# A decoder trunk on one core: the bias rows of one head group stored once, the even mixer and the last tail in another order, and a pair's scores computed in two halves of the array

## The chip, the core and the metric

The kernel runs on one core of one Trainium2 chip. The core has five engines with instruction streams of their own: TensorE (PE; the profile lists its weight loads apart, as PEld), VectorE (DVE), ScalarE (ACT), GpSimd (POOL) and SyncE (SP), which here only issues DMAs. The metric is device microseconds of one execution. Three runs of the kernel before gave 584.12 us as their median (583.64 to 584.29). The profiled execution took 583.38 us; its span, from the first to the last thing that the profiler recorded, is 581.6 us, so 1.8 us lie around it.

## The reference, cut to what matters

256 tokens of width 1024, four residual layers, each with an RMSNorm in front:

- an even mixer: one input projection; half of its output goes through a double-gated convolution of width 3, half through causal pooling means over 2, 4, 8 and 16 tokens with a linear map per group; both halves are concatenated and projected back;
- a gated MLP of 2816 with a causal convolution of width 3 before SiLU;
- an odd mixer: 16 heads of width 64. Heads 0 to 7 add a difference of cumulated forget gates to the logits, heads 8 to 15 add a bias by distance, `rel_bias[bucket(q - k)]` (T5's buckets). All are causal. The softmax over keys and the product with the values follow, then the output projection;
- a second gated MLP, and a last RMSNorm over each token.

For heads 8 to 15 the bias of query q and key k depends on q - k alone, so one row of 256 numbers per head holds all of it.

## The kernel before, in words

Everything is float32. Each operand of a large product is split into a rounded part (`hi`, type fp32r) and a rest (`lo`), and three products replace one: hi·hi, hi·lo, lo·hi (`mm3`, L276). Weights come in blocks of 128x1024: SP issues the DMA into `st` (eight buffers), ACT casts it to `hi` (L133), DVE subtracts it for `lo` (L134); seven pairs of buffers hold the split blocks. `ahead()` (L154) keeps six blocks on the way beyond the one in use, in the order of the list `blocks`, which is written out at L73 to L121.

The order of PE's instructions is the order of the program (`manual_schedule` with `ORDERED`). The order on ACT, DVE and POOL is set by a planner, except in the first loads (L257) and in the end of the kernel (`ordered_final`, L845), where ACT and DVE keep the order of the program too.

**Even mixer** (L396 to L512). Four groups j of 128 channels. `even_in("x", j)` and `even_in("y", j)` project; from the results `pool_sums`, `pool_less` and `pool_map` make `yb[j]`, and `conv_half` makes `ya[j]`. `even_add(j)` adds the output projection of `ya[j]` and then of `yb[j]`, 24 matmuls each. The PSUM pool `psA` hands out four banks in turn.

**First MLP** (`ffn`, L517). Its `aside` is `t5_rows` (L584): a small matmul makes the bias rows of the eight heads, DVE copies them into `row` (8 partitions x 384, the last 128 columns a large number), and POOL issues one DMA that writes each row 128 times into DRAM (`rowd`, 8x128x384).

**Odd mixer** (L600 to L813). Heads go in pairs p. `pair_bias` (L661) reads a 128x2x256 tile per pair: for heads 8 to 15 from `rowd` with a step of 383 per partition, so that each partition sees its row shifted by one. `queries` and `keys` project with 24 matmuls of 256 columns each. `part_keys` (L696) splits the keys of both heads into the tile `kz`, in which the other head's 64 partitions are zero (memsets at L693, L694, on POOL). `scores` (L702) then runs three matmuls of 512 columns (queries 128 to 255, both heads' 256 keys side by side) and three of 256 (queries 0 to 127, 128 keys each). DVE adds the bias and takes the extreme (L716, L718), ACT takes exponentials. Two pairs later PE transposes the result (`turn`, L733), and `mix` (L745) multiplies it by the values, one head into partitions 0 to 63 of `po` and one into 64 to 127.

**End** (`final`, L816). The last MLP accumulates by token: `acc.t[i][n]` holds tokens 128i to 128i+127 and columns 512n to 512n+511. The last two blocks of the output weights are kept as `tail`; for i and n in turn the tail's products close a bank, ACT squares and sums it (L834), DVE multiplies by the norm's weights (L836), and after n = 1 the row's scale is made (L838, L839 on POOL), applied (L840 on DVE, L841 on ACT) and the halves are sent (L842 on ACT's queue, L843 on SP's).

Of the kernel before, what the change touches and what calls it, by code (L numbers as in the profile page):

```python
# [11 lines left out]
F32 = mybir.dt.float32  # L12
# [27 lines left out]
SPLIT = 7  # L40
LOOK = 6
LEAD = 8
FIRST = LEAD + T + 512

# [6 lines left out]
def trunk(ctx, tc, a, out):  # L51
# [25 lines left out]

    def even_in_blocks(j):
        for n, kind in enumerate("xy"):
            for q in range(2):  # L80
                block(("e" + kind, j, q), a["ev_in"][GROUPS[j], n, :, q * BLK:(q + 1) * BLK])

    def even_out_blocks(j):
        block(("eo", j), a["ev_out"][GROUPS[j]])
        block(("eo", j + NG), a["ev_out"][GROUPS[j] + NG])

    for j in range(1, NG):
        even_in_blocks(j)
        if j >= 2:
            even_out_blocks(j - 2)  # L90
    even_out_blocks(NG - 2)
    even_out_blocks(NG - 1)

    def ffn_blocks(l):
        for kind, f in ffn_steps:
# [5 lines left out]
        for f in (NF - 2, NF - 1):  # L101
            block(("fo", l, f), a["ff_out"][l, f])
# [293 lines left out]
    with tc.tile_pool(name="ev", bufs=2) as ev, tc.tile_pool(name="evc", bufs=1) as evc:  # L396
# [46 lines left out]

        def even_add(j, between=None):
            acc.add_all(weights(("eo", j)), ya[j])
            if between is not None:
                between()
            acc.add_all(weights(("eo", j + NG)), yb[j])

# [45 lines left out]
        ahead()  # L495
        even_add(0, lambda: pool_map(1))
        ahead()
        zx = even_in("x", 3)
        pool_sums(3, zx[:, 0, :])
        pool_map(2)  # L500
# [16 lines left out]
    def ffn(l, st, hg, ps_z, ps_acc, kind_acc, end, aside=None):  # L517
        with tc.tile_pool(name=f"ff{l}", bufs=2) as fp:
            acc = None
            ready = {}  # L520
            rrow = None
            z0 = None

# [22 lines left out]

            for kind, f in ffn_steps:
# [30 lines left out]
            tail = [(weights(("fo", l, k)), ready.pop(k)) for k in (NF - 2, NF - 1)]  # L578
            return end(acc, tail)


    rowd = drp.tile([NH, P, 384], F32, name="rowd")

    def t5_rows(ps):  # L584
# [15 lines left out]
    with tc.tile_pool(name="od", bufs=2) as od, tc.tile_pool(name="odc", bufs=1) as odc:  # L600
# [60 lines left out]
        def pair_bias(p):  # L661

            b = od.tile([P, 2, T], F32, tag="bias", name="bias", bufs=3)
            if p < 4:
                s = fd[:, :]
                src = bass.AP(tensor=s.tensor, offset=s.offset + 2 * p * T, ap=[[0, P], [T, 2], [1, T]])
            else:
                s = rowd[:, :, :]
# [22 lines left out]
        kzs = [odc.tile([P, 2, 2, T], F32R, name=f"kz{i}") for i in range(2)]  # L691
        for kz in kzs:
            nc.gpsimd.memset(kz[HD:, :, 0, :].bitcast(F32), 0.0)  # L693
            nc.gpsimd.memset(kz[:HD, :, 1, :].bitcast(F32), 0.0)  # L694

        def part_keys(kz, kf):  # L696
            for s in range(2):
                r = slice(s * HD, (s + 1) * HD)
                nc.scalar.copy(kz[r, 0, s, :], kf[r, :])
                nc.vector.tensor_sub(kz[r, 1, s, :], kf[r, :], kz.bitcast(F32)[r, 0, s, :])  # L700

        def scores(qs, kz, bias):  # L702

            pr2 = []
            sums = []
            ps1 = psB.tile([P, 2, T], F32, tag="ps", name="ps_s1")
            ps0 = psB.tile([P, 2, T], F32, tag="ps", name="ps_s0")
            for n, (x, y) in enumerate(((0, 0), (0, 1), (1, 0))):
                nc.tensor.matmul(ps1, qs[x][:, P:], kz[:, y], start=n == 0, stop=n == 2)
            for n, (x, y) in enumerate(((0, 0), (0, 1), (1, 0))):  # L710
                nc.tensor.matmul(ps0[:, :, :P], qs[x][:, :P], kz[:, y, :, :P], start=n == 0, stop=n == 2)
            for s in range(2):
                n1, n0 = bias[s]
                lg = od.tile([P, 384], F32, tag="lg", name="lg")
                mx = od.tile([P, 2], F32, tag="mx", name="mx")
                nc.vector.tensor_tensor_reduce(lg[:, :T], ps1[:, s, :], n1, 1.0, 3e38, op0=ALU.add, op1=ALU.min,  # L716
                                               accum_out=mx[:, 0:1])
                nc.vector.tensor_tensor_reduce(lg[:, T:], ps0[:, s, :P], n0, 1.0, 3e38, op0=ALU.add, op1=ALU.min,  # L718
                                               accum_out=mx[:, 1:2])
# [43 lines left out]

        def keys(p, kz, between=None):
# [8 lines left out]
        qs, pr, pb, turned = {}, {}, {}, {}  # L773

        def score(i):
            pr[i] = scores(qs.pop(i), kzs[i % 2], pb.pop(i))

# [8 lines left out]
        for i, p in enumerate(order):  # L786
            pb[i] = bias_of(p)
            qs[i] = queries(p, lambda: turn_at(i - 2))
            if i >= 1:
                score(i - 1)  # L790
            keys(p, kzs[i % 2], lambda: mix_at(i - 2))
            if i == 0:
# [23 lines left out]
    def final(acc, tail):  # L816
        with tc.tile_pool(name="fin", bufs=1) as fin:
# [10 lines left out]

            for i in range(2):
                r, v = rcol[:, i:i + 1], var[:, i:i + 1]  # L830
                for n in range(2):
                    for m, (w, y) in enumerate(tail):
                        acc.add(i, n, w, y, m == len(tail) - 1)
                    nc.scalar.activation(junk, acc.t[i][n], AF.Square, accum_out=sums[:, i, n:n + 1])  # L834
                    if n == 0:
                        nc.vector.tensor_mul(hg_[:, i, :], acc.t[i][0], gb[:, :512])  # L836
                        nc.vector.tensor_scalar(v, sums[:, i, 0:1], 1.0 / D, EPS, op0=ALU.mult, op1=ALU.add)
# [22 lines left out]
def _layout(i):  # L860
# [40 lines left out]
    hot = np.zeros((32, T), np.float32)  # L901
    hot[_t5_bucket()[::-1], np.arange(T)] = -1.0
    a["hot"] = hot
# [20 lines left out]
```

## Time and profile before

| what | value |
|---|---|
| median of three runs | 584.12 us (583.64 to 584.29) |
| profiled execution | 583.38 us |
| its span | 581.6 us |
| granted clock of TensorE, mean over the span | 0.994 |
| ACT busy, DVE busy | 350.3 us, 453.8 us |
| PE's share of the chain that ended last | 71% |
| matmuls | 3696 |

Busy time of PE is from modelled ends of pipelined matmuls: one row's duration overlaps the next. What a matmul costs is read from the distance between starts. `L301` is line 301 of the kernel; `zg<-hg,hi` is the tile written and the tiles read, buffer numbers left out; `128*128` are the rows and columns of the array in use; "idle before" names what ended an engine's idle time. The granted clock is 1.00 at 2.4 GHz and 0.50 at 1.2 GHz.

### The profile page before, as it was taken

To read this page: it belongs to the slowest core of one execution; us is meant where nothing else is said; L and a number is where in the kernel's file an instruction comes from. 1 tells how busy PE (TensorE), PEld (TensorE's weight loads), DVE (VectorE), ACT (ScalarE), POOL (GpSimd) and SP (SyncE) were. 2 spreads that over 40 slices of the span, in tenths; PEclk is the share of its full clock that TensorE was granted. 3 is DMA by queue.
4 is the path that set the end of the run, shared out by engine and by line. 5 is a ranking of instruction groups with operands and counts; after the bars stand their busy time and mean duration, and the time that the engine had idled before them with its cause. 6 is when DMAs were issued, how large, how long until landed. Compare 5 with 4: busy or idle time off the path is not lost.

```text
span 581.6 us, 9818 instructions
## 1 busy us (share of the span) xinstructions
PE 568.8 (98%) x3696; PEld 512.4 (88%) x3696; DVE 453.8 (78%) x784; ACT 350.3 (60%) x618; POOL 79.1 (14%) x91
## 2 busy tenths in 40 slices
PE   8999999998999999999999999999999999999995
PEld 7999998997999999999888999998888888888883
DVE  6999698944999777878688888578977787887752
ACT  7764476623667555557567776566755556555532
POOL 1531051000000000004171347031000000000000
PEclk9999999998999999999999999999999999999998
DMA  8966636578777655655656443447465555656001
GB/s 311 405 219 202 233 117 215 90 138 249 265 237 220 190 188 186 190 185 152 228 179 185 159 152 112 147 142 245 156 197 195 181 188 183 189 187 202 1 2 72
DMA packets 30896, 106.00 MB, mean 182 GB/s; under 512 B 4112, under 2 KB 4376, under 8 KB 30848
## 3 DMA queue, kind: packets, MB, share of 16 engines
q1 hardware_dynamic: 28944, 100.61, 52.8%
q0 software_dynamic: 1616, 4.24, 4.2%
q8 instruction: 29, 0.48, 0.3%
q10 hardware_dynamic: 288, 0.52, 0.2%
q14 instruction: 19, 0.16, 0.1%
HBM read 102.72 MB, written 2.63 MB: 181 GB/s over the span
## 4 chain that ended last, share of the span: by engine, by line
PE 71%; issue 9%; DMA 7%; DVE 6%; POOL 4%; ACT 1%; SPq 0%; POOLq 0%; ACTq 0%
PE zg L301 12%; PE zu L301 12%; PE zg L302 6%; PE zu L302 6%; DMA st<-in_ff_out 5%; PE acc L278 4%; PE acc L279 4%; PE acc L277 4%; PE ta L279 3%; PE ta L278 3%; PE ta L277 3%; DVE lo L134 2%; POOL nb L677 1%; PE pv L615 1%; PE pv L617 1%
## 5 line engine op out<-in xcount | busy, mean ns | idle before, releaser
L134 DVE TENSOR_TENSOR lo<-st,hi 128x1024 fp32r<-128x1024 f32 (+1 forms) x186 | 230.2, 1246 | 80.5 <-ACT hi L133 79.3
L133 ACT CAST hi<-st 128x1024 fp32r<-128x1024 f32 (+1 forms) x186 | 191.9, 1039 | 124.8 <-PE acc L278 22.0
L301 PE MATMUL zg<-hg,hi 128*128 128x512 f32 x352 | 127.9, 401 | 2.5 <-DVE zs L533 2.5
L301 PE MATMUL zu<-hg,hi 128*128 128x512 f32 x352 | 126.3, 397 | 0.3 <-DVE hg L197 0.3
L302 PE MATMUL zg<-hg,lo 128*128 128x256 f32 x352 | 99.3, 282 | 0.0
L302 PE MATMUL zu<-hg,lo 128*128 128x256 f32 x352 | 98.7, 280 | 0.0
L301 PEld LDWEIGHTS zg<-hg,hi 128*128 128x128 f32 x352 | 66.7, 190 | 18.5 <-DVE zs L533 2.8
L301 PEld LDWEIGHTS zu<-hg,hi 128*128 128x128 f32 x352 | 66.1, 188 | 15.9 <-DVE hg L197 0.6
L302 PEld LDWEIGHTS zu<-hg,lo 128*128 128x128 f32 x352 | 66.6, 189 | 0.8
L302 PEld LDWEIGHTS zg<-hg,lo 128*128 128x128 f32 x352 | 67.2, 191 | 0.0
L279 PE MATMUL acc<-y_h,lo 128*128 128x256 f32 x176 | 49.6, 282 | 0.0
L277 PE MATMUL acc<-y_h,hi 128*128 128x256 f32 x176 | 49.6, 282 | 0.0
L278 PE MATMUL acc<-y_l,hi 128*128 128x256 f32 x176 | 49.5, 281 | 0.0
L310 ACT CAST y_h<-y 128x256 fp32r<-128x256 f32 x44 | 17.8, 406 | 38.3 <-DVE y L544 38.3
L388 ACT ACTIVATE t<-zs,vec 128x256 f32<-128x256 f32 x44 | 26.4, 601 | 15.7 <-DVE zs L537 15.7
L217 POOL TENSOR_TENSOR sqs<-sq 128x512 f32<-128x512 f32 x4 | 5.2, 1294 | 223.9 <-ACT sq L212 223.9
L277 PE MATMUL ta<-hi,y_h 128*128 128x512 f32 x88 | 34.8, 395 | 0.0
L279 PE MATMUL ta<-hi,y_l 128*128 128x512 f32 x88 | 34.7, 395 | 0.0
L278 PE MATMUL ta<-lo,y_h 128*128 128x512 f32 x88 | 34.7, 395 | 0.0
L277 PEld LDWEIGHTS acc<-y_h,hi 128*128 128x128 f32 x176 | 33.1, 188 | 0.8
L279 PEld LDWEIGHTS acc<-y_h,lo 128*128 128x128 f32 x176 | 33.2, 188 | 0.0
L278 PEld LDWEIGHTS acc<-y_l,hi 128*128 128x128 f32 x176 | 33.1, 188 | 0.0
(222 smaller groups left out, 1211.3 us busy)
## 6 DMA issues: line engine op xcount, KB each, us to landing
st<-in_ff_in SPq DMA_DIRECT2D x88, 512.0 KB, 4.4
st<-in_ff_out SPq DMA_DIRECT2D x44, 512.0 KB, 4.3
st<-in_od_qk SPq DMA_DIRECT2D x16, 512.0 KB, 4.3
st<-in_ev_in SPq DMA_DIRECT2D x10, 512.0 KB, 7.1
st<-in_ev_out SPq DMA_DIRECT2D x8, 512.0 KB, 3.9
st<-in_od_v SPq DMA_DIRECT2D x8, 512.0 KB, 3.6
st<-in_od_out SPq DMA_DIRECT2D x8, 512.0 KB, 3.9
first<-in_first SPq DMA_DIRECT2D x7, 388.0 KB, 6.0
```

What stands on the lines that cost most here:

```text
L133: nc.scalar.copy(hi[:, s:e], st[:, s:e])
L134: nc.vector.tensor_sub(lo[:, s:e], st[:, s:e], hi.bitcast(F32)[:, s:e])
L277: nc.tensor.matmul(o, wh, xh, start=start, stop=False, skip_group_check=skip)
L278: nc.tensor.matmul(o, wh, xl, start=False, stop=False, skip_group_check=skip)
L279: nc.tensor.matmul(o, wl, xh, start=False, stop=stop, skip_group_check=skip)
L301: nc.tensor.matmul(z, wh, x[:, k], start=first, stop=False, skip_group_check=True)
L302: nc.tensor.matmul(z[:, 1, :], wl, x[:, k, 0, :], start=False, stop=last, skip_group_check=True)
L310: nc.scalar.copy(hi, src)
L388: nc.scalar.activation(t, u, AF.Identity, scale=col(w0 + 2), bias=bias)
L615: nc.tensor.matmul(pv[i], xh, wh, start=k == 0, stop=False)
L617: nc.tensor.matmul(pv[i], xl, wh, start=False, stop=k == NK - 1)
L677: nc.gpsimd.tensor_scalar(nb[:, T:], fbh[:, :P], fq[:, hh:hh + 1], None, op0=ALU.subtract)
```

## The change

Four things. The T5 rows are written once (`rowd` is 8x384), with the large number in front and the row's distances rising behind it; each partition q reads from offset q on, which gives the keys last first, and DVE reads the tile backwards. In the even mixer the output projections of `ya[j]` and `yb[j]` are added separately, and the x projection of group 3 runs between those of group 0; the weight blocks follow that order. The last MLP keeps three blocks for the tail (`TAIL`), and in the end the first bank of tokens 128 to 255 is closed before tokens 0 to 127 are scaled and sent, both halves of which then go out on SP's queue. `scores` no longer uses `kz`: the keys are split once for both heads (`split`), and each head's products use only its own 64 partitions, into a bank of its own.

```diff
@@ even mixer's blocks and program
+    even_in_blocks(1)
+    even_in_blocks(2)
+    even_out_block(0)
+    even_in_blocks(3, "x")
+    even_out_block(NG)
+    even_in_blocks(3, "y")
     for j in range(1, NG):
...
+        even_out_block(j)
+        even_out_block(j + NG)
...
-        even_add(0, lambda: pool_map(1))
-        ahead()
+        even_add(0)
+        pool_map(1)
         zx = even_in("x", 3)
         pool_sums(3, zx[:, 0, :])
+        ahead()
+        even_add(NG)
         pool_map(2)
-        ahead()
         zy = even_in("y", 3)
         conv_half(3, zx, zy)
         pool_less(3)
         ahead()
         even_add(1)
+        even_add(NG + 1)
         pool_map(3)
-        ahead()
         even_add(2)
-        ahead()
+        even_add(NG + 2)
@@ last MLP
+TAIL = 3
+    last_steps = ffn_steps + [("out", f) for f in range(NF - LAG, NF - TAIL)]
...
+            steps, n = ((ffn_steps, 2), (last_steps, TAIL))[l]
...
+            tail = [(weights(("fo", l, k)), ready.pop(k)) for k in range(NF - n, NF)]
@@ rows
-    rowd = drp.tile([NH, P, 384], F32, name="rowd")
+    rowd = drp.tile([NH, 384], F32, name="rowd")
...
-        nc.gpsimd.memset(row[:, T:], BIG)
-        nc.vector.tensor_copy(row[:, :T], prow[:NH, :T])
-        nc.gpsimd.dma_start(rowd, row[:, None, :].to_broadcast([NH, P, 384]))
+        nc.gpsimd.memset(row[:, :P - 1], BIG)
+        nc.vector.tensor_copy(row[:, P - 1:383], prow[:NH, :T])
+        nc.gpsimd.memset(row[:, 383:], BIG)
+        nc.gpsimd.dma_start(rowd, row)
...
-                src = bass.AP(tensor=s.tensor, offset=s.offset + 127 + (2 * p - NH) * P * 384,
-                              ap=[[383, P], [P * 384, 2], [1, T]])
+                src = bass.AP(tensor=s.tensor, offset=s.offset + (2 * p - NH) * 384, ap=[[1, P], [384, 2], [1, T]])
...
-            return [(b[:, s, :], b[:, s, P:]) for s in range(2)]
+            return [(b[:, s, ::-1], b[:, s, P - 1::-1]) for s in range(2)]
@@ scores
-            for n, (x, y) in enumerate(((0, 0), (0, 1), (1, 0))):
-                nc.tensor.matmul(ps1, qs[x][:, P:], kz[:, y], start=n == 0, stop=n == 2)
-            for n, (x, y) in enumerate(((0, 0), (0, 1), (1, 0))):
-                nc.tensor.matmul(ps0[:, :, :P], qs[x][:, :P], kz[:, y, :, :P], start=n == 0, stop=n == 2)
+            ps = [psB.tile([P, 512], F32, tag="ps", name=f"ps_s{s}") for s in range(2)]
+            for q, e in ((slice(P, T), slice(0, T)), (slice(0, P), slice(T, T + P))):
+                for n, (x, y) in enumerate(((0, 0), (0, 1), (1, 0))):
+                    for s in range(2):
+                        r = slice(s * HD, (s + 1) * HD)
+                        nc.tensor.matmul(ps[s][:, e], qs[x][r, q], ks[y][r, :e.stop - e.start], start=n == 0, stop=n == 2)
...
-            part_keys(kz, kf)
             ahead()
+            return split(od, kf, None, "ks")
@@ end
+            def products(i, n):
+                for m, (w, y) in enumerate(tail):
+                    acc.add(i, n, w, y, m == len(tail) - 1)
+                nc.scalar.activation(junk, acc.t[i][n], AF.Square, accum_out=sums[:, i, n:n + 1])
+                if n == 0:
+                    nc.vector.tensor_mul(hg_[:, i, :], acc.t[i][0], gb[:, :512])
+                    nc.vector.tensor_scalar(var[:, i:i + 1], sums[:, i, 0:1], 1.0 / D, EPS, op0=ALU.mult, op1=ALU.add)
+
+            def send(i, queue):
...
-                nc.scalar.dma_start(out[i, :, :512], o[:, i, :512])
+                queue.dma_start(out[i, :, :512], o[:, i, :512])
                 nc.sync.dma_start(out[i, :, 512:], o[:, i, 512:])
+
+            products(0, 0)
+            products(0, 1)
+            products(1, 0)
+            send(0, nc.sync)
+            products(1, 1)
+            send(1, nc.scalar)
```

The host's layout of `hot` follows the new order of the rows.

## Rows read from the trace of the kernel before

**Rows 1.** The page's first part: busy time, share of the span and instructions of each engine.

```profile
PE 568.8 (98%) x3696; PEld 512.4 (88%) x3696; DVE 453.8 (78%) x784; ACT 350.3 (60%) x618; POOL 79.1 (14%) x91
```

**Rows 2.** What PE waited for, longest first: total us, times, longest.

```profile
PE zg L301 <- DVE zs L533: 2.5, 1, 2.5
...
PE acc L278 <- DVE ybl L318: 0.9, 1, 0.9
```

**Rows 3.** DMA issues by line: queue, count, KB each, median us from issue to landing.

```profile
rowd<-row POOLq DMA_DIRECT2D x1, 1536.0 KB, 35.7
...
bias<-rowd POOLq DMA_DIRECT2D x4, 256.0 KB, 3.5
bias<-fd POOLq DMA_DIRECT2D x4, 256.0 KB, 4.2
```

**Rows 4.** The chain of work that ended last, in the first MLP: start us, us, what.

```profile
109.54 29.03 DMA st<-in_ff_out
...
138.65 1.05 ACT hi L133
```

**Rows 5.** PE in order of time around 140 us: start us, us, line, tile, array rows*columns, shape, idle before.

```profile
135.90 0.40 PE L301 MATMUL zu<-hg,hi 128*128 128x512 f32 x1
...
138.60 0.28 PE L302 MATMUL zu<-hg,lo 128*128 128x256 f32 x1
...
141.34 0.80 PE L301 MATMUL zg<-hg,hi 128*128 128x512 f32 x1 [2.46 <-DVE zs L533]
...
145.54 0.28 PE L277 MATMUL acc<-y_h,hi 128*128 128x256 f32 x1
```

**Rows 6.** Three stretches of the first MLP: us, busy time (instructions) of PE, PEld, DVE, ACT and POOL, then the granted clock of TensorE, the mean busy share of the DMA engines, and GB/s.

```profile
100.00:138.00 38.00, 38.00 (x249) 34.55 (x248) 23.80 (x42) 16.99 (x31) 1.15 (x1) 1.00 0.63 119
138.00:141.30 3.30, 0.88 (x6) 0.52 (x4) 1.56 (x2) 2.33 (x3) 0.00 (x0) 0.93 0.91 355
141.30:144.20 2.90, 2.86 (x9) 2.47 (x10) 2.85 (x5) 1.58 (x3) 0.00 (x0) 0.50 0.82 305
```

**Rows 7.** PE in order of time in the even mixer, where the projection of `yb[0]` begins.

```profile
44.67 0.28 PE L277 MATMUL acc<-ybh,hi 128*128 128x256 f32 x1
45.80 0.39 PE L278 MATMUL acc<-ybl,hi 128*128 128x256 f32 x1 [0.85 <-DVE ybl L318]
46.03 0.27 PE L279 MATMUL acc<-ybh,lo 128*128 128x256 f32 x1
```

**Rows 8.** DVE in order of time in the same stretch.

```profile
34.31 1.22 DVE L134 TENSOR_TENSOR lo<-st,hi 128x1024 fp32r<-128x1024 f32 x1
...
43.07 0.41 DVE L433 TENSOR_TENSOR cv<-zx,rrow 128x256 f32<-128x256 f32 x1
...
45.27 0.48 DVE L318 SCALAR_TENSOR_TENSOR ybl<-zp,vec,ybh 128x256 fp32r<-128x256 f32 x1
```

**Rows 9.** PE in order of time: the first matmuls of one pair's scores and the first matmul behind its six.

```profile
304.16 0.63 PE L709 MATMUL ps_s<-kz,qsh 128*128 128x512 f32 x2
...
305.22 0.28 PE L277 MATMUL zk<-hg,hi 128*128 128x256 f32 x1
```

**Rows 10.** PE in order of time around `mix`, whose matmuls use 64 of the array's columns each; those of its first line in the code, four, stand in one merged line.

```profile
314.77 0.28 PE L279 MATMUL zk<-hg,lo 128*128 128x256 f32 x1
314.98 0.66 PE L750 MATMUL po<-ptb,va 128*64 128x256 f32 x4
...
315.79 0.39 PE L277 MATMUL zk<-hg,hi 128*128 128x256 f32 x1
316.01 0.28 PE L278 MATMUL zk<-hg,hi 128*128 128x256 f32 x1
```

**Rows 11.** Busy time and, in brackets, instructions of line 750 alone that run within 40 ns: PE, PEld, granted clock, DMA share, GB/s.

```profile
314.97:315.01 0.04, 0.03 (x2) 0.03 (x2) 1.00 0.00 0
```

**Rows 12.** PE in order of time: two of the 128-column transposes of `turn`.

```profile
319.15 0.27 PE L737 MATMUL ps_t<-ident,pr 128*128 128x128 f32 x1
319.26 0.27 PE L738 MATMUL ps_t<-ident,pr 128*128 128x128 f32 x1
```

**Rows 13.** Groups by line, engine and shape in the odd mixer: busy us, mean ns of one, idle before.

```profile
L700 DVE TENSOR_TENSOR kz<-kf,kz 64x256 fp32r<-64x256 f32 x16 | 8.2, 513 | 0.3
...
L716 DVE CUSTOM_DVE_ANT_0 lg<-ps_s,bias 128x256 f32<-128x256 f32 x8 | 3.4, 420 | 1.1 <-PE ps_s L709 1.1
```

**Rows 14.** PE, ACT and DVE in order of time in the last 12 us.

```profile
571.64 0.60 ACT L834 ACTIVATE junk<-ta 128x512 f32<-128x512 f32 x1 [0.77 <-PE ta L279]
...
572.37 0.16 DVE L838 SCALAR_TENSOR_TENSOR var<-sums,var 128x1 f32<-128x1 f32 x1 [0.70 <-ACT junk L834]
...
573.19 0.73 ACT L841 ACTIVATE o<-hg__6697,rcol 128x512 f32<-128x512 f32 x1 [0.86 <-POOL rcol L839]
...
573.94 0.40 PE L279 MATMUL ta<-hi,y_l 128*128 128x512 f32 x1
...
574.39 0.60 ACT L834 ACTIVATE junk<-ta 128x512 f32<-128x512 f32 x1 [0.47 <-PE ta L279]
...
575.11 0.60 ACT L834 ACTIVATE junk<-ta 128x512 f32<-128x512 f32 x1
575.11 0.69 DVE L836 TENSOR_TENSOR hg__6697<-ta,gb 128x512 f32<-128x512 f32 x1 [1.17 <-ACT junk L834]
...
575.97 0.16 DVE L838 SCALAR_TENSOR_TENSOR var<-sums,var 128x1 f32<-128x1 f32 x1
```

More of the change, by code (lines that the diff above doesn't have):

```diff
@@ L76, in block, with even_in_blocks, even_out_block @@
         blocks.append((key, src))
-    def even_in_blocks(j):
-        for n, kind in enumerate("xy"):
+    def even_in_blocks(j, kinds="xy"):
+        for kind in kinds:
             for q in range(2):
[L81 to L85, printed above, removed]
-    for j in range(1, NG):
[L88 to L92, printed above, removed]
+                block(("e" + kind, j, q), a["ev_in"][GROUPS[j], "xy".index(kind), :, q * BLK:(q + 1) * BLK])
+    def even_out_block(j):
+        block(("eo", j), a["ev_out"][GROUPS[j % NG] + j // NG * NG])
+    even_in_blocks(1)
[4 more added lines that the diff above has]
+    even_in_blocks(3, "y")
+    for j in range(1, NG):
+        even_out_block(j)
+        even_out_block(j + NG)
     def ffn_blocks(l):
-        for kind, f in ffn_steps:
+        steps, n = ((ffn_steps, 2), (last_steps, TAIL))[l]
+        for kind, f in steps:
             if kind == "in":
@@ L100, in ffn_blocks @@
                 block(("fo", l, f), a["ff_out"][l, f])
-        for f in (NF - 2, NF - 1):
+        for f in range(NF - n, NF):
             block(("fo", l, f), a["ff_out"][l, f])
@@ L442, in conv_half, with even_add @@
             ya[j] = split(ev, y, None, "ya", bufs=4)
[L444 to L448, printed above, removed]
+        def even_add(j):
+            acc.add_all(weights(("eo", j)), ya[j] if j < NG else yb[j - NG])
+            ahead()
         rows_box = []
@@ L495, in trunk @@
         ahead()
-        even_add(0, lambda: pool_map(1))
-        ahead()
+        even_add(0)
+        pool_map(1)
         zx = even_in("x", 3)
         pool_sums(3, zx[:, 0, :])
+        ahead()
+        even_add(NG)
         pool_map(2)
-        ahead()
         zy = even_in("y", 3)
@@ L521, in ffn @@
             rrow = None
-            z0 = None
+            early = []
             def new_z():
@@ L545, in gate @@
                 ready[f] = split(fp, y, None, "y_", bufs=LAG + 2)
-            for kind, f in ffn_steps:
+            steps, n = ((ffn_steps, 2), (last_steps, TAIL))[l]
+            for kind, f in steps:
                 if kind == "out":
@@ L577, in ffn @@
                     aside(ps_acc)
-            tail = [(weights(("fo", l, k)), ready.pop(k)) for k in (NF - 2, NF - 1)]
+            tail = [(weights(("fo", l, k)), ready.pop(k)) for k in range(NF - n, NF)]
             return end(acc, tail)
-    rowd = drp.tile([NH, P, 384], F32, name="rowd")
+    rowd = drp.tile([NH, 384], F32, name="rowd")
     def t5_rows(ps):
@@ L687, in bias_of, with scores @@
                 return [fox_bias(2 * p + s, b[:, s, :]) for s in range(2)]
-            return [(b[:, s, :], b[:, s, P:]) for s in range(2)]
[L691 to L702, printed above, removed]
+            return [(b[:, s, ::-1], b[:, s, P - 1::-1]) for s in range(2)]
+        def scores(qs, ks, bias):
             pr2 = []
             sums = []
-            ps1 = psB.tile([P, 2, T], F32, tag="ps", name="ps_s1")
-            ps0 = psB.tile([P, 2, T], F32, tag="ps", name="ps_s0")
-            for n, (x, y) in enumerate(((0, 0), (0, 1), (1, 0))):
-                nc.tensor.matmul(ps1, qs[x][:, P:], kz[:, y], start=n == 0, stop=n == 2)
-            for n, (x, y) in enumerate(((0, 0), (0, 1), (1, 0))):
-                nc.tensor.matmul(ps0[:, :, :P], qs[x][:, :P], kz[:, y, :, :P], start=n == 0, stop=n == 2)
+            ps = [psB.tile([P, 512], F32, tag="ps", name=f"ps_s{s}") for s in range(2)]
[4 more added lines that the diff above has]
+                        nc.tensor.matmul(ps[s][:, e], qs[x][r, q], ks[y][r, :e.stop - e.start], start=n == 0, stop=n == 2)
             for s in range(2):
@@ L715, in scores @@
                 mx = od.tile([P, 2], F32, tag="mx", name="mx")
-                nc.vector.tensor_tensor_reduce(lg[:, :T], ps1[:, s, :], n1, 1.0, 3e38, op0=ALU.add, op1=ALU.min,
+                nc.vector.tensor_tensor_reduce(lg[:, :T], ps[s][:, :T], n1, 1.0, 3e38, op0=ALU.add, op1=ALU.min,
                                                accum_out=mx[:, 0:1])
-                nc.vector.tensor_tensor_reduce(lg[:, T:], ps0[:, s, :P], n0, 1.0, 3e38, op0=ALU.add, op1=ALU.min,
+                nc.vector.tensor_tensor_reduce(lg[:, T:], ps[s][:, T:T + P], n0, 1.0, 3e38, op0=ALU.add, op1=ALU.min,
                                                accum_out=mx[:, 1:2])
@@ L762, in queries, with keys @@
             return split(od, qf, None, "qs")
-        def keys(p, kz, between=None):
+        def keys(p, between=None):
             z = psA.tile([P, 512], F32, tag="ps", name="zk")
@@ L768, in keys @@
             nc.vector.tensor_mul(kf, z[:, :T], rrow)
-            part_keys(kz, kf)
             ahead()
-        qs, pr, pb, turned = {}, {}, {}, {}
+            return split(od, kf, None, "ks")
+        qs, ks, pr, pb, turned = {}, {}, {}, {}, {}
         def score(i):
-            pr[i] = scores(qs.pop(i), kzs[i % 2], pb.pop(i))
+            pr[i] = scores(qs.pop(i), ks.pop(i), pb.pop(i))
         def turn_at(i):
@@ L790, in trunk @@
                 score(i - 1)
-            keys(p, kzs[i % 2], lambda: mix_at(i - 2))
+            ks[i] = keys(p, lambda: mix_at(i - 2))
             if i == 0:
@@ L827, in final @@
             rcol = fin.tile([P, 2], F32, name="rcol")
-            for i in range(2):
-                r, v = rcol[:, i:i + 1], var[:, i:i + 1]
[L831 to L837, printed above, removed]
+            def products(i, n):
[6 more added lines that the diff above has]
+            def send(i, queue):
+                r, v = rcol[:, i:i + 1], var[:, i:i + 1]
                 nc.vector.scalar_tensor_tensor(v, sums[:, i, 1:2], 1.0 / D, v, op0=ALU.mult, op1=ALU.add)
@@ L901, in _layout @@
     hot = np.zeros((32, T), np.float32)
-    hot[_t5_bucket()[::-1], np.arange(T)] = -1.0
+    hot[_t5_bucket(), np.arange(T)] = -1.0
     a["hot"] = hot
```

2 lines of the change are left out of this document (1 added, 1 removed).

## The prediction

> **What bounds the kernel now.** First the page's busy times: PE is busy 98% of the span [rows 1]. Its ends are modelled, so the second view is what PE waited for; the reader should see how little there is, with one wait of 2.5 us and one of 0.9 us as the only ones beyond the first microseconds that this change can touch [rows 2]. So time is won in two ways only: by taking a PE wait away, or by giving PE's queue less to run. Work of ACT, DVE, POOL or the DMAs counts where PE ends up waiting for it. The third view, the first MLP in order of time, tells what the 2.5 us were: one 512 KB weight block took 29.03 us to land [rows 4], while the store of the T5 rows, 1536 KB in 35.7 us, was under way [rows 3]; in that stretch the DMA engines moved 119 GB/s [rows 6]. ACT stood before that block's cast, and the evacuation of PE's banks stood behind the cast in ACT's queue, so PE stopped with it.
>
> **The rows, stored once.** The store falls from 1536 KB to 12 KB, so the slow block should land like its neighbours. What it cost PE: eight pairs of matmuls for `zu` ran from 135.90 to 138.72 (the last start, 138.60, and 0.12), 2.82 us. The eight of `zg` would then have ended at 141.54; the next product begins at 145.54 [rows 5]. The loss is 4.0 us. 2.5 of it is the wait; the rest is the clock: after those idle microseconds the granted clock was 0.50, that is 1.2 GHz, from 141.3 to 144.2 [rows 6]. I take all of it, 4.0 us; the other end is 0, if something else holds the block up.
>
> The reads keep their 1024 KB. All partitions now read out of the same three kilobytes; the nearest row is the gate bias, which broadcasts one row and lands in 4.2 us against 3.5 [rows 3]. I take +0.7 us each; they are requested well before use and PE waits for none of them today, so it sees nothing. Backward reading on DVE has no row. Forward the addition takes 420 ns [rows 13]; I take the same. If it doubled, each of the four pairs would be 4 x 0.42 = 1.7 us longer at most, on DVE, whose results the transposes two pairs later want. On POOL one memset becomes two, and the four for `kz` go.
>
> **The even mixer.** PE should have started the second product of `yb[0]` at 44.79, and started at 45.80, because DVE delivered `ybl` late; the next one came 0.11 us late as well [rows 7]. With the 48 matmuls of x3 in between (48 x 0.12 = 5.8 us), `ybl`, done at 45.75 [rows 8], is wanted at 50.5. Gain 1.1 us. What is late next: x3 now begins at 44.7, four microseconds earlier. Its weights are cast: the twelfth block, the second of x3, was split on DVE by 35.5 [rows 8], and on SP's queue and in the casts it moves up by a place. Its bank is the one of x2, which DVE reads last at 43.07 to 43.48 [rows 8]: 1.2 us to spare, but behind a DVE queue whose order the planner sets. If that read slips by two microseconds, most of the gain is gone. I take -1.1, range -1.1 to 0.
>
> **The scores.** Before, six matmuls take 305.22 - 304.16 = 1.06 us per pair, 2304 columns in all, so 0.118 us per 256 columns [rows 9]. After, twelve: six of 256 columns and six of 128, each on 64 rows of the array, the two heads in turn. If the halves run side by side there are three slots of 0.118 and three of 128 columns. A 128-column slot is not half a 256 one: transposes of 128 columns start 0.11 us apart [rows 12]. That makes 0.69 us.
>
> Do halves run side by side? No row shows 64 rows. The nearest is `mix`, 64 columns each: two heads' matmuls are both running within the first 40 ns [rows 11]. But that row also shows a price. From the last `zk` before `mix` to the second one behind it 1.24 us pass [rows 10]; take off the two ordinary matmuls (0.24) and the work itself (passes of 256 and 128 columns, float32 in two passes each at about twice the time: 0.2 + 0.2 + 0.1 + 0.1, about 0.62), and 0.36 us are left for going into the smaller shape and out again. With that the scores take 0.69 + 0.36 = 1.05 us, against 1.06. So I expect almost nothing: -0.02 a pair, -0.2 us over eight. Both ends: no price for the shape, 0.69, is -0.37 a pair or -2.9 us; halves one after the other, 6 x 0.118 + 6 x 0.11 + 0.36 = 1.73, is +0.67 a pair or +5.3 us. I stay with the value nearest to the row of `mix`.
>
> On the row of `mix` alone halving the array buys nothing here; the Trainium skill (TensorEngine Tiling (Array Packing), Theoretical Speedup) gives up to 2x for a contraction of 64 or less, which would make the scores 0.53 us and the total 4.2 us shorter. The same page (Key Properties) says that a change of tiling mode drains the engine, and the 0.36 us in the trace agree.
>
> Per pair the split of the keys falls from two ACT and two DVE instructions (DVE 513 ns each [rows 13]) to one and one. PE never waits for them, so they count as nothing, except that they give DVE half a microsecond a pair of slack.
>
> **The end.** Three blocks in the tail leave PE's total as it is. What counts is ACT's order. Now the last bank is ready at about 574.4 (last start 573.94 plus its columns), but ACT squares (1,0) first, as it had waited for the scale of tokens 0 to 127 and issued a DMA, and starts the last square at 575.11 [rows 14]. After: groups are of nine matmuls, 2.1 us, so (1,0) closes at 572.3. Square and sum take 0.7, to 573.0; DVE's multiplication waits for that, as it does now at 575.11; the sum for tokens 0 to 127 is queued behind it on DVE, at 573.8. From there to ACT's scaling is 0.82 (572.37 to 573.19), so 574.6; it lasts 0.73 and stands before the last square, which starts at 575.4. From square to DVE's sum is 0.73, so 576.1 against 575.97 [rows 14]. I take +0.1 us. Ends: -0.7 if the scaling were out of the way (575.11 back to 574.4), +0.9 if two output halves on SP, sent about 1.5 us later than now, get into the last transfer's way.
>
> **The sum.** -4.0 - 1.1 - 0.2 + 0.1 = -5.2 us. On the profiled execution that is 583.4 - 5.2 = 578.2; the median lies 0.7 above it, so 584.1 - 5.2 = 578.9.
>
> **Rivals.**
> 1. The halves take turns without further loss: +5.3 instead of -0.2, total +0.3, 584.4. For it: no row has 64 rows. Against: `mix`. A milder form ends near it: the matmuls overlap but the weight loads don't, twelve loads at the 0.11 of [rows 12] plus 0.36 make 1.68, +5.0 over eight pairs, 584.1. For that form speaks the Trainium skill (TensorE: Matmul & The Clock Gate, LDWEIGHTS): the price of a load goes by its columns, not its rows, so a half load is no cheaper. Chance of the two 0.15.
> 2. Slower than before: every change between the halves costs what leaving `mix` costs. The second `zk` starts 0.22 us after the first instead of 0.12 (315.79 to 316.01 [rows 10]). Twelve matmuls at 0.22 make 2.64, +1.6 a pair, +12.7 in all, 584.1 - 5.0 + 12.7 = 591.8. It decides from 0.8 us a pair on, which is 0.15 us per matmul. Against: the halves in `mix` alternate too. Chance 0.06.
> 3. The shape costs nothing on rows: -2.9 instead of -0.2, 576.2. For it: the tax is shown on columns only. Chance 0.13.
> 4. The rows don't do what they say: the block is slow for another reason and PE stops as now, 584.1 - 1.2 = 582.9. Against: the store's own 35.7 us and the 119 GB/s in just that stretch [rows 3, 6]. Chance 0.04.
>
> **How the numbers follow.** Forecast 0.62, the rivals 0.15, 0.06, 0.13, 0.04. No change, as a measurement of this kernel can tell it, is 0.2%, 1.2 us: 582.9 to 585.3. Faster: forecast, rival 3 and half of 4 and a part of 1, 0.79. Same: most of 1 and the rest of 4, 0.15. Slower: 0.06. The range reaches from rival 3 up to half-way between forecast and rival 1, where even mixer or shape give less: 576.0 to 583.0.
>
> **What would show it.** Rows: no load of a weight block anywhere near 29 us, PE's wait for `zs` gone, clock 1.00 throughout the first MLP. Even mixer: no wait for `ybl`, none for `cv` before x3. Scores: from the first of the twelve to the first `zk` behind them; 1.05 is my value, 0.7 is rival 3, 1.7 rival 1, 2.6 rival 2; and whether two of them start some 15 ns apart. End: the last square about 1.0 us behind the last matmul's end. The prediction is wrong if the scores' stretch is off by 0.3 us a pair, or a new PE wait stands in the first MLP or before x3.

## The result and the profile after

The changed kernel takes 577.83 us, median of 4 runs (577.50 to 578.16), against 583.88 (583.59 to 584.29) for the kernel before: a ratio of 0.9895, 95% interval 0.988 to 0.991. The profiled execution took 577.5 us; its span is 575.7 against 581.6, at a mean granted clock of 0.998 against 0.994. The prediction was 578.9 (576.0 to 583.0).

The page of the changed kernel: its span, the busy line that answers to [rows 1], and the shares of the chain that ended last.

```profile
span 575.7 us, 9890 instructions
...
PE 566.7 (98%) x3744; PEld 510.8 (89%) x3744; DVE 452.3 (79%) x776; ACT 346.3 (60%) x610; POOL 74.4 (13%) x88
...
PE 96%; DVE 1%; issue 1%; POOL 0%; DMA 0%; ACT 0%; POOLq 0%; ACTq 0%; SPq 0%
```

PE was busy 98% of the span before and is so after; that share tells nothing. The chain tells it: 96% of it is PE now, 71% before. Next PE's waits, longest first, which answer to [rows 2] (total us, times, longest).

```profile
PE pwarm L176 <- DVE mhalf L183: 1.2, 1, 1.2
PE zu L306 <- DVE hg L202: 0.7, 2, 0.4
```

The waits for `zs` and `ybl` are gone. The first line is the start, the same in both kernels. The second is the news: PE now waits twice for `hg`, the scaled input of an MLP, and only once before, at the second MLP. In the kernel before that wait and one for `pr`, the scaled probabilities, stood in the same list:

```profile
PE ps_t L737 <- DVE pr L730: 0.3, 1, 0.3
PE zu L301 <- DVE hg L197: 0.3, 1, 0.3
```

Then the stores and reads of the T5 rows, which answer to [rows 3], and the clock in the last two stretches of [rows 6].

```profile
bias<-rowd POOLq DMA_DIRECT2D x4, 256.0 KB, 4.0
bias<-fd POOLq DMA_DIRECT2D x4, 256.0 KB, 3.6
...
rowd<-row POOLq DMA_DIRECT2D x1, 12.0 KB, 1.7
```

```profile
138.00:141.30 3.30, 3.30 (x24) 2.97 (x23) 1.99 (x3) 1.95 (x3) 0.00 (x0) 1.00 0.56 168
141.30:144.20 2.90, 2.90 (x24) 2.81 (x23) 2.25 (x3) 1.38 (x3) 0.00 (x0) 1.00 0.63 195
```

The store fell from 35.7 us to 1.7. PE is busy throughout both stretches, 24 matmuls in each where 6 and 9 ran, at a clock of 1.00 where it was 0.93 and 0.50.

To share the 5.9 us out, take the start of a named matmul in both traces and subtract:

| first matmul of | before | after | shift | what lies in between |
|---|---|---|---|---|
| x of group 1, even mixer | 17.43 | 17.05 | -0.38 | start-up, unchanged code |
| first MLP | 77.93 | 76.45 | -1.49 | even mixer: -1.11 |
| T5 rows (`prow`) | 95.70 | 94.62 | -1.08 | the new wait for `hg`: +0.41 |
| values (`pv`) | 270.16 | 265.21 | -4.95 | the stall around 140: -3.87 |
| scores of pair 0 | 304.16 | 299.34 | -4.82 | +0.13: the scores' first matmul starts 0.09 later than an ordinary one, small waits 0.04 |
| scores of pair 1 | 312.40 | 306.95 | -5.45 | mainly a wait for probabilities: -0.60; scores -0.03 |
| odd mixer's output | 359.89 | 354.19 | -5.71 | pairs 1 to 6: -0.26, of it -0.09 the late start that the two rows above carry |
| last matmul of all | 573.94 | 568.14 | -5.79 | -0.09: pair 7 -0.03, second MLP -0.06 |
| end of the span | 581.6 | 575.7 | -5.9 | the end: -0.1 |

Two lines in it were in no term of the prediction: +0.41 and -0.60. For the second, PE in order of time at the transposes of pair 0, before and then after:

```profile
310.01 0.27 PE L739 MATMUL ps_t<-ident,pr 128*128 128x128 f32 x1
310.58 0.33 PE L737 MATMUL ps_t<-ident,pr 128*128 128x128 f32 x1 [0.30 <-DVE pr L730]
```

```profile
304.80 0.27 PE L733 MATMUL ps_t<-ident,pr 128*128 128x128 f32 x1
305.06 0.33 PE L731 MATMUL ps_t<-ident,pr 128*128 128x128 f32 x1
```

From head 0's last transpose to head 1's first 0.57 us pass before and 0.26 after; another 0.2 went at head 0's first (0.32 behind the last `zq`, now 0.12). PE waited for the scaled probabilities of the first pair; they come sooner now.

### The profile page after: what moved, and what is told of

Its sections match the earlier page's. It is cut to its first block, busy times and chain, and to the rows that moved or that the text cites. A ratio compares the mean times of both kernels' runs of the same rounds, so it can differ in the third digit from the quotient of the medians.

```text
span 575.7 us, 9890 instructions
## 1 busy us (share of the span) xinstructions
PE 566.7 (98%) x3744; PEld 510.8 (89%) x3744; DVE 452.3 (79%) x776; ACT 346.3 (60%) x610; POOL 74.4 (13%) x88
## 4 chain that ended last, share of the span: by engine, by line
PE 96%; DVE 1%; issue 1%; POOL 0%; DMA 0%; ACT 0%; POOLq 0%; ACTq 0%; SPq 0%
PE zu L306 14%; PE zg L306 14%; PE zg L307 7%; PE zu L307 7%; PE acc L282 6%; PE acc L284 6%; PE acc L283 6%; PE ta L284 3%; PE ta L283 3%; PE ta L282 3%; PE zk L282 2%; PE zq L282 1%; PE zq L283 1%; PE zk L284 1%; PE zq L284 1%; PE zk L283 1%
## 5 line engine op out<-in xcount | busy, mean ns | idle before, releaser
L139 DVE TENSOR_TENSOR lo<-st,hi 128x1024 fp32r<-128x1024 f32 (+1 forms) x186 | 229.8, 1242 | 76.9 <-ACT hi L138 75.3
```

Source lines behind the costliest of these rows:

```text
L139: nc.vector.tensor_sub(lo[:, s:e], st[:, s:e], hi.bitcast(F32)[:, s:e])
```

## The experiments

The first four do one part of the change alone, on the kernel before. They were measured beside 25 runs of the kernel before: median 583.66 us, 581.96 to 585.56.

**rows_only.** The rows stored once, nothing else.

```diff
-    rowd = drp.tile([NH, P, 384], F32, name="rowd")
+    rowd = drp.tile([NH, 384], F32, name="rowd")
-        nc.gpsimd.dma_start(rowd, row[:, None, :].to_broadcast([NH, P, 384]))
+        nc.gpsimd.dma_start(rowd, row)
...
+            return [(b[:, s, ::-1], b[:, s, P - 1::-1]) for s in range(2)]
```

> The kernel before with the rows stored once and nothing else. My theory: the 4.0 us that PE lost around 140 us (wait and low clock) go, and nothing else moves: about 579.9 us, no matmul at the 1.2 GHz level in the first MLP. Rival: the stall came from PE being late elsewhere, or the even mixer's reordering is needed for it too: 582 us or more and a wait of PE for zs that stays.

Measured: 579.53 us (579.39 to 580.16), ratio 0.9937 [0.9923, 0.9952]. PE's wait for `zs` is gone; the matmuls of the table up to `prow` lie within 0.03 us of the kernel before, all those behind the stall 3.85 to 3.91 earlier. So the stall cost 3.9 us, wait and clock together, and the backward reading gives none of it back. Its four runs also spread less: 0.8 us, against 3.6 in 25 runs of the kernel before and 2.2 to 2.5 in ten of each of the three next kernels, which keep the old store. The spread goes with the clock: the eight of the 25 with a mean granted clock of 0.996 or 0.997 took 581.96 to 583.15 us, the seventeen with 0.994 or 0.995 took 583.38 to 585.56. The profiled one, with 0.994, is one of the latter kind.

**scores_only.** The keys split once for both heads, twelve matmuls on 64 rows each, no `kz` and none of its four memsets.

```diff
-        for kz in kzs:
-            nc.gpsimd.memset(kz[HD:, :, 0, :].bitcast(F32), 0.0)
-            nc.gpsimd.memset(kz[:HD, :, 1, :].bitcast(F32), 0.0)
...
+                        nc.tensor.matmul(ps[s][:, e], qs[x][r, q], ks[y][r, :e.stop - e.start], start=n == 0, stop=n == 2)
```

> The kernel before with the keys split once and the scores in two halves, nothing else. My theory: 1.03 us per pair against 1.06, -0.2 us in all, plus up to 0.6 us where PE waited for the first pair's probabilities, since ACT and DVE have one instruction less each: 583.0 to 583.7 us. Rival: halves are worth the factor of two that half a contraction promises, -4 us: 580.

Measured: 583.03 us (581.51 to 584.01), ratio 0.9994 [0.9981, 1.0006]. In its trace the first MLP loses 0.31 us to the new wait for `hg`, pair 0 gains 0.62, pairs 1 to 6 gain 0.26 (with the 0.09 of the late start, as in the table). So both unforeseen lines of the table are this part's. 1.3 us more in that one execution come from the stall at 140 us: PE waits 2.4 us there, 2.5 before, but behind the wait the granted clock stays at 1.00, where it fell to 0.50 before.

**even_only.** The even mixer's new order alone.

```diff
-        even_add(0, lambda: pool_map(1))
-        ahead()
+        even_add(0)
+        pool_map(1)
         zx = even_in("x", 3)
         pool_sums(3, zx[:, 0, :])
+        ahead()
+        even_add(NG)
```

> The kernel before with the even mixer's new order alone. My theory from the two traces: the 1.1 us at the wait for ybl are won and about 0.4 us are given back where the first MLP begins, since PE now arrives there before DVE has the last of hg: 583.2 us. Rival: all of the 1.1 us stays: 582.8 us or less, and no wait of PE for hg before 90 us.

Measured: 582.14 us (580.98 to 583.26), ratio 0.9974 [0.9962, 0.9986]. My theory was wrong: I had taken the new wait for `hg` to come with the earlier start of the MLP, and there is none here. The table's matmuls are 0.20 early from the start-up on, 1.30 at the MLP's start and 1.28 at `prow`: 1.1 us, and all of it kept up to there. Behind the stall 0.75 is left, as the stall was 0.5 longer in this execution.

**end_only.** Three blocks in the tail and the new order in the end.

```diff
+            products(0, 0)
+            products(0, 1)
+            products(1, 0)
+            send(0, nc.sync)
+            products(1, 1)
+            send(1, nc.scalar)
```

> The kernel before with the tail of three blocks and the new order of the end alone. My theory: the last square still waits behind the scaling of the other tokens on ACT, so the end moves by -0.1 to +0.1 us: 583.8 to 584.0 us. Rival: the last square follows the last matmul at once, -0.7 us: 583.2 us.

Measured: 582.74 us (581.90 to 584.09), ratio 0.9987 [0.9973, 1.0001]. The times don't decide, since they carry the stall's spread. The trace does: from the last matmul's start to the end of the span 7.5 us (574.09 to 581.6), against 7.7 before. The end is worth -0.1 to -0.2.

**halves_in_turn.** The changed kernel, but PE's queue holds three matmuls of the first head and then three of the second, not the two in turn.

```diff
-                for n, (x, y) in enumerate(((0, 0), (0, 1), (1, 0))):
-                    for s in range(2):
-                        r = slice(s * HD, (s + 1) * HD)
+                for s in range(2):
+                    r = slice(s * HD, (s + 1) * HD)
+                    for n, (x, y) in enumerate(((0, 0), (0, 1), (1, 0))):
```

> The changed kernel with one head's three products first and then the other's, so that no two neighbouring matmuls use different halves. My theory: side by side is what holds the scores at 1.03 us a pair, and the change of shape costs 0.34 of it; in turn, 3 slots more of 0.115 and of 0.06 to 0.10 us each: 1.5 to 1.7 us a pair, +4 to +5 us in all, about 582. Rival: the order doesn't matter, since the queue lets the second head's matmuls pass: 577.8, 1.03 us a pair.

Measured: 578.72 us (578.21 to 578.89), ratio 0.9913 [0.9881, 0.9945]: 0.6 to 0.9 above the changed kernel's two medians (577.83 and 578.10), not 4 to 5. From the first score matmul to the first `zk` 0.84 us pass, as in the changed kernel, and within the first 40 ns two matmuls of the scores run. First PE in order of time, then the 40 ns (PE and PEld busy, with instructions in brackets, then clock, DMA share and GB/s):

```profile
299.96 0.39 PE L705 MATMUL ps_s<-ksh,qsh 64*128 64x256 f32 x2
300.19 0.29 PE L705 MATMUL ps_s<-ksl,qsh 64*128 64x256 f32 x2
...
299.96:300.00 0.04, 0.04 (x2) 0.04 (x2) 1.00 1.08 435
```

A head has only one product of each pair of tiles and size, so the two in a line are one of each head; they start 8 to 14 ns apart, all the way. The theory that the order makes the halves overlap is wrong: the second head's first matmul starts ahead of two matmuls of the first head that stand before it in the queue.

**store_128, store_64, store_wide.** The changed kernel, and a store into a scratch tensor that nobody reads, written in the program right behind the small one: as large as the old one, half as large, and as large again but in two DMAs from all 128 partitions.

```diff
         nc.gpsimd.dma_start(rowd, row)
+        probe = drp.tile([NH, P, 384], F32, name="probe")
+        nc.gpsimd.dma_start(probe, row[:, None, :].to_broadcast([NH, P, 384]))
```

```diff
         nc.gpsimd.dma_start(rowd, row)
+        probe = drp.tile([P, 12, T], F32, name="probe")
+        nc.gpsimd.dma_start(probe[:, :8, :], h)
+        nc.gpsimd.dma_start(probe[:, 8:, :], h[:, :4, :])
```

(store_64 has `64` for `P` in the first.)

> The changed kernel, with the old store of 128 copies per row (1536 KB from 8 partitions) added into an unused tensor. My theory: the stall comes back as it was: landing about 36 us, a weight block that takes over 20 us to land, PE's wait of about 2.5 us and the 1.2 GHz stretch, 581.5 us. Rival: it was the layout that was read later, not the store: 577.8.

> The changed kernel with 64 copies per row stored (768 KB). My theory: the weight loads fall behind at the same rate for half as long, some 18 us, and the blocks fetched ahead cover it: no PE wait, 577.8 us. Rival: the loss is in proportion to the bytes: +2 us, 579.8.

> The changed kernel with 1536 KB stored from 128 partitions (the residual, into an unused tensor) instead of from 8. My theory: it is the few engines behind 8 partitions that hold the weights up, not the bytes: it lands in 5 to 10 us, no PE wait, 577.8 us. Rival: bytes written to DRAM are the price: landing above 20 us and the wait of 2.5 us back, 581.5.

Measured, one run each: 581.32, 578.32 and 578.93 us. PE's waits, the chain of work that ended last and the DMA issues of store_128, then the issues of the other two:

```profile
PE zg L306 <- DVE zs L537: 2.9, 1, 2.9
...
107.76 30.45 DMA st<-in_ff_out
...
probe<-row POOLq DMA_DIRECT2D x1, 1536.0 KB, 35.8
```

```profile
probe<-row POOLq DMA_DIRECT2D x1, 768.0 KB, 18.5
```

```profile
probe<-h POOLq DMA_DIRECT2D x1, 1024.0 KB, 4.2
...
probe<-h POOLq DMA_DIRECT2D x1, 512.0 KB, 5.0
```

The big store alone brings the wait back, 2.9 us, with a weight block of 30.45 us beside it. The stretch at 1.2 GHz, which the theory also wanted, is missing: the granted clock stays at 1.00 behind the wait, and from `prow` to `pv` this trace is 3.1 us longer than the changed kernel's, not 3.9. Half of the store takes half the time; no block takes longer than 17.9 us beside it, and PE doesn't wait.

store_wide does not answer its question. POOL's order is set by the planner, and it issued the two stores at 75.3 and 79.2 us, where store_128 went out at 102.4 and store_64 at 103.0. Hardly a load was under way there: after_again moves 0 to 15 GB/s from 78 to 84 us. So it is shown that the old store makes the wait, and that half of it doesn't. Whether that lies in its 8 partitions, in its short runs or only in its 36 us beside the weights, no run separates. The Trainium skill (DMA: Bandwidth & Descriptors, Why a DMA increments its semaphore by 16 and not by 1) says that a DMA is dealt out over the largest number of engines, 16 at most, that divides the slowest dimension of both its sides, which by that rule would be 8 here; no run shows it.

The last four kernels were measured on one chip, beside 7 runs of the kernel before (583.64 us, 582.30 to 584.37). **after_again** is the changed kernel once more.

> The changed kernel itself, as the control of the other three runs on the same chip: 577.8 us, within 577.4 to 578.2.

Measured: 578.10 us (577.70 to 578.36), ratio 0.9909 [0.9892, 0.9926].

**sums_on_dve.** For the +0.41. DVE and POOL in order of time around the last `hg` of the first MLP, in the kernel before and in the changed one (start us, us; two `hg` instructions stand in one line):

```profile
80.53 1.97 DVE L197 SCALAR_TENSOR_TENSOR hg<-h,vec,hg 128x256 fp32r<-128x256 f32 x2 [0.42 <-ACT hg L196]
...
80.31 0.53 POOL L693 MEMSET kz<- 64x512 f32 x1
80.92 1.29 POOL L217 TENSOR_TENSOR sqs<-sqs,sq 128x512 f32<-128x512 f32 x1
```

```profile
79.04 2.81 DVE L202 SCALAR_TENSOR_TENSOR hg<-h,vec,hg 128x256 fp32r<-128x256 f32 x2 [0.42 <-ACT hg L201]
...
78.74 1.28 POOL L222 TENSOR_TENSOR sqs<-sqs,sq 128x512 f32<-128x512 f32 x1
...
80.27 1.29 POOL L222 TENSOR_TENSOR sqs<-sqs,sq 128x512 f32<-128x512 f32 x1
```

Two `hg` take 0.87 us where POOL is idle. Before, the second of them lay under one addition of POOL; the first ran beside a memset and was not held. Without the memsets of `kz` POOL reaches its additions sooner, two of them lie over the two `hg`, and each waits: 79.04 to 81.85, 0.3 us behind the end of POOL's second addition (80.27 + 1.29 = 81.56). PE would have wanted the second one at 81.4 and starts at 81.90. The experiment takes POOL's additions away:

```diff
-                nc.gpsimd.tensor_add(s, self.sum, sq)
+                engine.tensor_add(s, self.sum, sq)
...
-            st.feed(b)
+            st.feed(b, engine=nc.vector)
```

> The changed kernel with the boundary's additions of sums of squares on DVE in place of POOL. Theory: DVE's last two hg instructions at the start of the first FFN are stretched to 2.8 us because POOL's additions run beside them since the four kz memsets are gone from POOL; with no such POOL work hg takes about 0.5 us, PE's two waits for it at each FFN's start go (0.3 to 0.4 each, and a slow start behind it), 0.5 to 1.1 us in all, less what one 0.69 us addition between the hg instructions costs: 576.7 to 577.5 us. Rival: hg's length has nothing to do with POOL, or DVE's own additions make it as late: hg stays at 2 to 2.8 us, or the wait stays, 577.8 us or more.

Measured: 577.40 us (576.90 to 577.87), ratio 0.9898 [0.9880, 0.9915]. The medians are 0.70 us below the control and their ranges overlap a little; the trace is clear. DVE in order of time:

```profile
78.34 0.68 DVE L222 TENSOR_TENSOR sqs<-sq 128x512 f32<-128x512 f32 x1
79.05 0.89 DVE L202 SCALAR_TENSOR_TENSOR hg<-h,vec,hg 128x256 fp32r<-128x256 f32 x2
```

`hg` takes 0.89 for two, both waits of PE are gone, and against the control the first MLP gains 0.48 up to `prow` and the second 0.35 up to its tail. So the theory holds: POOL's additions make `hg` late. The Trainium skill (SBUF — State Buffer, Who interferes with whom) says that a DVE instruction with two inputs in SBUF and a POOL instruction that reads SBUF exclude each other, and one that only writes does not; addition and memset above agree with it.

**mix_next.** A pair's `mix` right behind the next pair's scores, so that two small shapes are neighbours.

```diff
                 score(i - 1)
-            ks[i] = keys(p, lambda: mix_at(i - 2))
+            mix_at(i - 2)
+            ks[i] = keys(p)
```

> The changed kernel with a pair's mix right behind the scores of the next pair, ahead of the keys' projection. Theory: the price of a small shape, about 0.34 us for each pair's scores, is paid for leaving the full array and coming back, so two small shapes that are neighbours share it: six of the seven mixes lose 0.2 to 0.34 us each, 1.2 to 2 us in all, 575.8 to 576.7 us. Rival 1: each change of shape has the same price, whatever the shape before: 577.8 us. Rival 2: the turned probabilities come too late for the earlier place, and PE waits on them: over 578 us, with a wait of PE at mix's first matmul.

Measured: 576.94 us (576.79 to 577.28), ratio 0.9891 [0.9872, 0.9911], 1.16 below the control. PE in order of time around `mix` in the changed kernel, then from the scores through `mix` in this one:

```profile
309.20 0.28 PE L284 MATMUL zk<-hg,lo 128*128 128x256 f32 x1
309.41 0.66 PE L744 MATMUL po<-ptb,va 128*64 128x256 f32 x4
...
310.22 0.39 PE L282 MATMUL zk<-hg,hi 128*128 128x256 f32 x1
310.44 0.28 PE L283 MATMUL zk<-hg,hi 128*128 128x256 f32 x1
```

```profile
307.27 0.28 PE L284 MATMUL zq<-hg,lo 128*128 128x256 f32 x1
307.48 0.38 PE L705 MATMUL ps_s<-ksh,qsh 64*128 64x256 f32 x2
...
308.11 0.28 PE L705 MATMUL ps_s<-ksh,qsl 64*128 64x128 f32 x2
308.32 0.66 PE L744 MATMUL po<-ptb,va 128*64 128x256 f32 x4
308.80 0.40 PE L745 MATMUL po<-ptb,va 128*64 128x128 f32 x4
309.12 0.39 PE L282 MATMUL zk<-hg,hi 128*128 128x256 f32 x1
309.35 0.28 PE L283 MATMUL zk<-hg,hi 128*128 128x256 f32 x1
```

From the last `zq` to the second `zk` behind both shapes 2.08 us pass; apart, scores and `mix` take 1.27 + 1.24 = 2.51, in which two ordinary matmuls (0.24) are counted twice: 2.27. The gain is 0.19 a pair, 1.1 us for six. That is a little less than the theory allowed (0.2 to 0.34 a pair), and it isn't quite the theory: I had named two cases, one price shared or nothing saved, and it is a third. `mix` starts 0.21 us behind the last score matmul, as `zk` did, so going from half the rows to half the columns is a change of shape like any other. Four changes a pair have become three, at some 0.19 each.

**both.** The two together.

> sums_on_dve and mix_next together. Theory: the two gains are at different places and add up: 574.7 to 576.5 us. Rival: one of the two is nothing, and the time is that of the better one alone.

Measured: 575.67 us (575.48 to 575.93), ratio 0.9869 [0.9852, 0.9885], 2.43 below the control; the two alone make 1.86. In its trace the start-up is 0.26 early, in unchanged code, which is part of the rest. This version beats both kernels: 8.0 us below the kernel before on the same chip, where the changed kernel is 5.5 below it.

## Why the prediction was right, step by step

- **Rows: right.** Forecast -4.0, shown -3.9 by rows_only alone, and that the old store makes the wait by store_128. The 4.0 is the price where the clock falls behind the wait; in the traces where it doesn't, the stall costs 2.6 (scores_only) and 3.1 (store_128). One link was left out: behind the cast the chain went through DVE's split of the block too (139.72 to 140.95), and only then to `zs`. The reads take 4.0 us, forecast 4.2, and no one waits for them. Backward reading costs what forward does, 417 ns against 420 in [rows 13]; the doubling that I kept as a bound doesn't occur. Rival 4 falls. The group of [rows 13] in the changed kernel:

```profile
L710 DVE CUSTOM_DVE_ANT_0 lg<-ps_s,bias 128x256 f32<-128x256 f32 x8 | 3.3, 417 | 0.0
```

- **Even mixer: right.** Forecast -1.1, shown -1.1 by even_only. `ybl` is written at 44.89 to 45.37 and wanted at 50.16. Nothing before x3 is late: the 1.2 us that I saw between its bank's last reader and its start held.
- **Scores: right in the sum, nearly right in the parts.** PE in order of time, where [rows 9] stood before:

```profile
299.13 0.28 PE L284 MATMUL zq<-hg,lo 128*128 128x256 f32 x1
299.34 0.38 PE L705 MATMUL ps_s<-ksh,qsh 64*128 64x256 f32 x2
299.56 0.28 PE L705 MATMUL ps_s<-ksl,qsh 64*128 64x256 f32 x2
299.68 0.28 PE L705 MATMUL ps_s<-ksh,qsl 64*128 64x256 f32 x2
299.80 0.23 PE L705 MATMUL ps_s<-ksh,qsh 64*128 64x128 f32 x2
299.86 0.28 PE L705 MATMUL ps_s<-ksl,qsh 64*128 64x128 f32 x2
299.97 0.28 PE L705 MATMUL ps_s<-ksh,qsl 64*128 64x128 f32 x2
300.18 0.39 PE L282 MATMUL zk<-hg,hi 128*128 128x256 f32 x1
300.40 0.28 PE L283 MATMUL zk<-hg,hi 128*128 128x256 f32 x1
```

Each line holds two matmuls, one of each head, 2 to 7 ns apart: the halves run side by side. From the first of them to `zk` it is 0.84 us; the first one comes 0.09 later than an ordinary matmul would and the second `zk` 0.10, which makes 1.03, against 1.06 before and 1.05 forecast. The work is 0.64 (0.12 three times, then 0.06, 0.11, 0.11) and not 0.69, since the first 128-column slot takes 0.06; the price of the shape is then 0.39 and not 0.36 (the prediction's own figures for `mix`, 1.24 - 0.24 - 0.62, leave 0.38). Over eight pairs -0.24, forecast -0.2. Rivals 1 to 3 (1.7, 2.6 and 0.7 us) fall. The argument against rival 2 was badly put, though: in `mix` the two heads do not alternate in PE's queue, each has its two matmuls in a row, and they ran at once all the same. halves_in_turn shows why this did no harm: in both orders tried the halves overlap.

- **The end: the sign was off, by 0.2.** ACT and DVE in the end, as in [rows 14]:

```profile
568.14 0.40 PE L284 MATMUL ta<-hi,y_l 128*128 128x512 f32 x1
568.75 0.72 ACT L836 ACTIVATE o<-hg__6728,rcol 128x512 f32<-128x512 f32 x1 [1.51 <-POOL rcol L834]
569.38 0.58 ACT L826 ACTIVATE junk<-ta 128x512 f32<-128x512 f32 x1
...
570.08 0.16 DVE L833 SCALAR_TENSOR_TENSOR var<-sums,var 128x1 f32<-128x1 f32 x1 [0.57 <-ACT junk L826]
```

The order is the one forecast: the scaling of tokens 0 to 127 stands before the last square. But the square starts 1.24 us behind the last matmul's start, where 1.46 was forecast (575.4 - 573.94) and 1.17 was measured before; DVE's sum follows at 1.94 instead of 2.16, against 2.03 before. The step "it lasts 0.73 and stands before the last square" is the mis-sized one: the next ACT instruction starts 0.63 behind it, since durations overlap, and distances between starts are what counts. The rest is rounding and 0.05 in the scaling's start.

- **What failed: "they count as nothing".** Two savings got no price. The memsets of `kz` on POOL have one: without them POOL's additions meet DVE's `hg`, and PE waits (+0.41). That it comes with the scores' part is shown by scores_only against even_only, that POOL's additions do it by sums_on_dve; that the missing memsets bring the additions forward is read from POOL's order in the two traces, and wasn't tried alone. By the prediction's own last line this is a sign of being wrong, "a new PE wait stands in the first MLP". And "PE never waits for them" was wrong for the first pair: `ps_t` waited for DVE's scaled probabilities, a row of 0.3 us in the list of PE's waits that I had passed over, and the shorter split of the keys took it away (-0.60, in scores_only too). Which of DVE's and ACT's saved instructions does it wasn't tried apart.
- **The sum.** Terms forecast: -5.2. Measured in the trace: -3.87 - 1.11 - 0.24 - 0.1 = -5.3 for the same terms, -0.60 and +0.41 for the two missed ones, -0.38 in the start-up, which no edit touches: -5.9, with small shifts that cancel. That the two missed terms nearly cancel is luck, and so is the start-up: in after_again the table's first matmul starts at 17.36, 0.07 early and not 0.38. The forecast lay 1.1 us high. 0.7 of that is in the profiled executions (578.2 forecast, 577.5 measured), by these terms; the other 0.4 is that the median lies 0.3 above the profiled execution after the change and not 0.7 as before it.

## What to carry to other kernels

When an instruction leaves an engine that isn't the bound, look at what moves up into its place and whom that meets: here a freed POOL held DVE up, and DVE held PE up. A change of the array's shape cost by the change here, not by the matmul, so put small shapes next to each other; whether each pays for itself is worked out with two changes a visit. A large store is judged by how long it is under way beside the loads: here the blocks fetched ahead covered 18.5 us of it and not 35.8. And look in the trace where an added instruction ran before reading anything from its time: store_wide ran elsewhere.

## What the runs showed of the hardware that I had not expected

- Matmuls on two halves of the rows overlap in both orders tried: the second half's first matmul started 10 ns behind the first half's, past two matmuls that stood before it (halves_in_turn). The Trainium skill (TensorE: Matmul & The Clock Gate, The mechanism) says that matmuls start strictly in the program's order; this trace shows otherwise for different halves.
- Each change of shape in the scores cost about 0.19 us: full array to 64 rows and back 0.39 in two, 64 rows to 64 columns one more of the same size (mix_next).
- DVE's `hg`, 0.87 us for two, is held for the length of POOL's additions, to 2.81, and not by POOL's memsets.
- 1536 KB out of 8 partitions took 35.8 us, and a 512 KB load beside it 30.45 instead of 4.2 (store_128); 768 KB took 18.5. 1024 and 512 KB out of 128 partitions took 4.2 and 5.0, but with hardly a load beside them (store_wide).
- Behind PE's wait at 140 us the granted clock fell to 0.50 for some 3 us in the kernel before (2.5 us of wait) and stayed at 1.00 in scores_only (2.4) and store_128 (2.9). What decides wasn't tried.
- Of three 128-column slots in the scores one takes 0.06 us and two 0.11. Why wasn't tried.
